# A decoder step's last down projection and final scaling in three token passes of 256, 192 and 128 instead of two of 320 and 256

## The chip, the cores and the metric

One Trainium2 chip, one of its cores. The metric is the device time of one execution in microseconds (us), the median of the runs; an execution also leaves a profile, whose times count from the start of its span. Engines: PE is TensorE (PEld its weight loads), DVE is VectorE, ACT is ScalarE, POOL is GpSimd, SP is SyncE.

## What is computed

One step of a decoder layer for 512 prompt tokens and 8 x 8 sample tokens (576 token columns), model width 1024, feed-forward width 3072, all in float32. The part that the change touches is the end of the layer and the norm behind it:

```
def rmsnorm(x, g):
    xf = x.astype(jnp.float32)
    y = xf * lax.rsqrt(jnp.mean(xf * xf, axis=-1, keepdims=True) + EPS)
    return (y * g.astype(jnp.float32)).astype(x.dtype)
...
    g_conv, new_ffn = causal_dwconv(g_pre, ffn_buf, lw['ffn_conv_w'], lw['ffn_conv_b'])
    h = h + (jax.nn.gelu(g_conv) * val) @ lw['w_down']
...
    y_prompt = rmsnorm(hp, g_final)
    y_sample = rmsnorm(hs, g_final)
```

Ahead of it stand the mixer branches (pooling, a recurrence with gates, cross-attention), their gated merge, and the up projection.

## The kernel before

Activations lie transposed, features on the 128 partitions and tokens along a row, so the model width is 8 tiles of 128 x 576 (`h[0]` to `h[7]`, slices of the one tile `S["h"]`). A float32 product is made of three matmuls of rounded operands (dtype float32r): high by high, high by low, low by high, where `split_to` (L111, L112) makes the high part on ACT and the low part on DVE. In such a matmul the weights are a 128x128 block and the tokens the columns that stream past it; each matmul has its own weight load (PEld).

The feed-forward part (`op_ffn`) runs over 24 tiles of the hidden width. The products of the up projection go into banks of PSUM (`bank()`, four of them, tile `pb`); the down projection is done in six groups of four hidden tiles. For the first five groups `down` (L989) does all 576 tokens in two halves of 288. The last group, `NGR - 1`, has nothing to hide behind and is done in token passes, which the table `FC` names: now columns 0 to 320 and 320 to 576. `last_mm(c, m)` does output tile m of pass c: 4 hidden tiles x 3 matmuls into one bank (L1138), then on DVE the sum with `h[m]` (L1143), on ACT the square of the sum (L277 in `SqSum.add`; L1150 for m = 7) and the scaling by the final norm's weight in place (L1152), and on POOL the running sum of squares (L279).

When a pass has its squares, `fin_cols` calls `rstd_cols`: matmuls with a column of ones, the squares as weights, make the sums over features as one column for each 128 tokens (L241, float32 operands, two matmul records for each instruction in the trace), and small steps on DVE and ACT make the reciprocal root (L245 to L253). `final(c)` spreads the root over the partitions by matmuls with the identity (L1165, float32 too), multiplies `h` by it on DVE, two output tiles at a time (L1172), and stores each result (L1173), in turn from the queues of SP and ACT. Sums, spreads and the bank that they go into come from `pq()`, which has two buffers (tile `pd`).

The order is that of the code, moved a little by the scheduler within the engines. The first pass's root is made and spread within the second pass:

```
        for m in range(8):
            last_mm(0, m)
        for m in range(7):
            last_mm(1, m)
            if m == 1:
                fin_cols(0)
            if m == 3:
                final(0)
        last_mm(1, 7)
        fin_cols(1)
        final(1)
```

Of the kernel before, what the change touches and what calls it, by code (L numbers as in the profile page):

```python
# [11 lines left out]
ALU = mybir.AluOpType  # L12
# [3 lines left out]
P = 128  # L16
# [32 lines left out]
def tile_hybrid_decoder_step(ctx: ExitStack, tc: tile.TileContext, A: dict):  # L49
    nc = tc.nc  # L50
# [16 lines left out]
    def nm(p):  # L67
        uid[0] += 1
        return f"{p}{uid[0]}{cur[0]}"
# [12 lines left out]
    def te(w=UW, dt=F32):  # L82
        if FF:
            return FF["v"].tile([P, T], dt, tag="v", name=nm("v"))[:, :w]
        return ue.tile([P, UW], dt, tag="e", name=nm("e"))[:, :w]
# [7 lines left out]
    def pq():  # L93
        if FF:
            return FF["d"].tile([P, 2, 512], F32, tag="d", name=nm("pd"))[:, 0, :]
        return psp.tile([P, 512], F32, tag="pq", name=nm("pq"), bufs=2)
# [131 lines left out]
    def pc(c):  # L228
        return par[:, c : c + 1]
# [64 lines left out]
    S = {}  # L294
# [428 lines left out]
    h = [None] * 8  # L723
# [23 lines left out]
    def op_ffn():  # L747
# [15 lines left out]
        def bank():  # L763
            return pb.tile([P, 512], F32, tag="b", name=nm("pb"))
# [302 lines left out]
        for j in range(NFF):  # L1067
            pre = j < NPRE
            g, q = j // NFB - 1, j % NFB
            n = j + 1  # L1070
# [53 lines left out]
            WD[last, q] = bt(2 * q, 1024), bt(2 * q + 1, 1024)  # L1124
            split_to(*WD[last, q], r)

        FC = (slice(0, 320), slice(320, 576))

        def last_mm(c, m):
            cs = FC[c]  # L1130
            n = cs.stop - cs.start
            wh, wl = WD[last, m // 2]
            p_ = bank()
            for k in range(NFB):
                xh, xl = prods[last * NFB + k]
                ks = slice((m % 2) * 512 + k * P, (m % 2) * 512 + (k + 1) * P)
                for i, (a, b) in enumerate(((wh, xh), (wh, xl), (wl, xh))):
                    nc.tensor.matmul(  # L1138
                        p_[:, :n], a[:, ks], b[:, cs],
                        start=(k == 0 and i == 0), stop=(k == NFB - 1 and i == 2),  # L1140
                    )
            hc = h[m][:, cs]
            nc.vector.tensor_tensor(hc, p_[:, :n], hc, ALU.add)  # L1143
            if m == 0:
                S["sqf", c] = SqSum(n)
            if m < 7:
                S["sqf", c].add(hc)
            else:
                s7 = te(n)
                nc.scalar.activation(s7, hc, AF.Square)  # L1150
                S["sq7", c] = s7
            nc.scalar.activation(hc, hc, AF.Identity, scale=pc(C_GFIN + m))  # L1152

        def fin_cols(c):
            cs = FC[c]
            S["fr", c] = rstd_cols((S["sqf", c].acc, S["sq7", c]), cs.stop - cs.start)

        def final(c):
            cs = FC[c]
            n = cs.stop - cs.start  # L1160
            r = S["fr", c]
            rl = pq()
            for t in range((n + P - 1) // P):
                w = min(P, n - t * P)
                nc.tensor.matmul(  # L1165
                    rl[:, t * P : t * P + w], r[:w, t : t + 1].to_broadcast([w, P]), ident[:w, :w],
                    start=True, stop=True,
                )
            for q_ in range(4):
                ms = slice(2 * q_, 2 * q_ + 2)  # L1170
                hc = S["h"][:, ms, cs]
                nc.vector.tensor_tensor(hc, hc, rl[:, :n].unsqueeze(1).to_broadcast([P, 2, n]), ALU.mult)  # L1172
                (nc.sync, nc.scalar)[q_ % 2].dma_start(A["yT"][:, ms, cs], hc)  # L1173

        for m in range(8):
            last_mm(0, m)
        for m in range(7):
            last_mm(1, m)
            if m == 1:
                fin_cols(0)  # L1180
            if m == 3:
                final(0)
        last_mm(1, 7)
        fin_cols(1)
        final(1)
        ff.close()


# [146 lines left out]
```

## Time and profile before

| | us |
|---|---|
| median of 3 runs (lowest to highest) | 944.61 (943.54 to 945.12) |
| the profiled execution | 942.23 |
| its span | 940.4 |
| PE busy in the span | 917.6 (98%) |
| DVE, ACT, POOL busy | 621.6, 471.4, 198.7 |
| first matmul of the last group (L1138) to the span's end | 902.2 to 940.4 |

The span is what the trace covers; what lies around it in the profiled execution is 942.23 - 940.4 = 1.8 us. A busy PE is not PE at its peak, since matmuls overlap and their ends are modelled: how fast a stream of matmuls runs is read from the distance of their starts. In a row of the timeline the numbers are the start in the span and the length in us, then engine, line, operation, tiles, shapes and count; in brackets is the idle time of the engine before it and what ended it.

### The profile page before, as it was taken

The page shows a single profiled execution, that of the slowest core. Times are in us where ns is not written, and L with a number is a line of the kernel's source. Part 1 is how long each engine was busy: PE and PEld are TensorE (multiplying, and loading weights), DVE is VectorE, ACT ScalarE, POOL GpSimd, SP SyncE. Part 2 cuts the span into 40 slices and gives each one's busy share as a digit, 9 for nine tenths or more (in the row PEclk, how much of TensorE's full clock was granted, in tenths as well). Part 3 has the DMA queues.
Part 4 walks back from the last instruction along what each step waited for, and adds up shares of the span by engine and source line. Part 5 has one row for each costly group of instructions (what it writes and reads, how often), then busy time and mean ns, then how long its engine had stood idle before and what let it go on. Part 6 is the DMA issues. An engine that isn't in the chain of part 4 may idle for free.

```text
span 940.4 us, 17089 instructions
## 1 busy us (share of the span) xinstructions
PE 917.6 (98%) x6924; PEld 902.1 (96%) x6924; DVE 621.6 (66%) x975; ACT 471.4 (50%) x745; POOL 198.7 (21%) x301
## 2 busy tenths in 40 slices
PE   6999999999999999999999999999999999999996
PEld 6999999999999979899999999999999999999996
DVE  7979864656434666237467998676676676676644
ACT  6455948496222546325455555444444444444443
POOL 5224221127113110012222232111111111111031
PEclk9999999999999999999999999999999999999998
DMA  6422222353232363433636355454454454453203
GB/s 236 141 79 68 70 77 69 95 166 131 87 113 83 124 227 121 175 114 113 223 80 147 100 160 154 125 145 135 125 145 136 127 143 135 126 144 102 90 33 101
DMA packets 39662, 116.73 MB, mean 124 GB/s; under 512 B 4608, under 2 KB 8704, under 8 KB 39584
## 3 DMA queue, kind: packets, MB, share of 16 engines
q1 hardware_dynamic: 34496, 100.19, 31.7%
q0 software_dynamic: 4000, 14.28, 8.7%
q8 instruction: 54, 0.88, 0.4%
q10 hardware_dynamic: 1088, 1.18, 0.4%
q14 instruction: 24, 0.20, 0.1%
HBM read 111.58 MB, written 4.05 MB: 123 GB/s over the span
## 4 chain that ended last, share of the span: by engine, by line
PE 87%; DVE 6%; issue 2%; DMA 2%; ACT 1%; POOL 1%; SPq 0%; POOLq 0%; DVEq 0%; ACTq 0%
PE pb_ffn L903 25%; PE ps_gate L199 15%; PE pd_ffn L989 13%; PE ps_branch L199 11%; PE pb_ffn L808 5%; PE ps_rnn_mm L199 3%; PE ps_q L199 3%; PE pb_ffn L1138 2%; PE ps_pool_mm L199 2%; PE pq_rnn_gate L199 1%; PE pq_k_mm L199 1%; PE ps_v L559 1%; DMA wr_start<-in_w_gate 1%; DMA cv_spv<-in_cv 1%; PE ps_pv L649 1%
## 5 line engine op out<-in xcount | busy, mean ns | idle before, releaser
L903 PE MATMUL pb_ffn<-b_ffn,wh_ffn 128*128 128x288 f32 x768 | 155.2, 295 | 0.0
L903 PEld LDWEIGHTS pb_ffn<-b_ffn,wh_ffn 128*128 128x128 f32 x768 | 123.3, 188 | 0.1
L903 PE MATMUL pb_ffn<-b_ffn,sh_ffn 128*128 128x288 f32 x576 | 119.3, 299 | 2.4 <-DVE b_ffn L112 1.3
L903 PE MATMUL pb_ffn<-b_ffn,wl_ffn 128*128 128x288 f32 x384 | 112.9, 294 | 0.0
L903 PEld LDWEIGHTS pb_ffn<-b_ffn,sh_ffn 128*128 128x128 f32 x576 | 92.1, 188 | 4.4 <-DVE b_ffn L112 1.7
L903 PE MATMUL pb_ffn<-b_ffn,sl_ffn 128*128 128x288 f32 x288 | 84.7, 295 | 0.2 <-DVE sl_ffn L112 0.2
L903 PEld LDWEIGHTS pb_ffn<-b_ffn,wl_ffn 128*128 128x128 f32 x384 | 72.2, 188 | 0.0
L111 ACT ACTIVATE wh_ffn<-wr_ffn 128x1024 fp32r<-128x1024 f32 x44 | 46.7, 1061 | 39.7 <-PE pb_ffn L903 37.7
L111 ACT ACTIVATE sh_ffn<-R_ffn 128x512 fp32r<-128x512 f32 x72 | 45.0, 626 | 26.3 <-PE pb_ffn L903 19.4
L989 PE MATMUL pd_ffn<-xb_ffn,wh_ffn 128*128 128x288 f32 x320 | 55.7, 295 | 1.0 <-ACT xb_ffn L111 1.0
L989 PE MATMUL pd_ffn<-xa_ffn,wh_ffn 128*128 128x288 f32 x320 | 55.7, 296 | 0.0
L903 PEld LDWEIGHTS pb_ffn<-b_ffn,sl_ffn 128*128 128x128 f32 x288 | 54.1, 188 | 0.4 <-DVE sl_ffn L112 0.4
L112 DVE TENSOR_TENSOR wl_ffn<-wr_ffn,wh_ffn 128x1024 fp32r<-128x1024 f32 x44 | 54.1, 1230 | 0.2
L111 ACT ACTIVATE wh_branch<-wr_branch 128x1024 fp32r<-128x1024 f32 (+1 forms) x24 | 22.0, 917 | 62.7 <-PE ps_gate L199 27.2
L976 POOL TENSOR_TENSOR v_ffn<-v_ffn,ext_ffn 128x576 f32<-128x576 f32 x24 | 35.9, 1498 | 79.8 <-ACT ext_ffn L965 77.2
L112 DVE TENSOR_TENSOR sl_ffn<-R_ffn,sh_ffn 128x512 fp32r<-128x512 f32 x72 | 51.3, 713 | 0.5 <-ACT sh_ffn L111 0.5
L112 DVE TENSOR_TENSOR wl_ffn<-R_ffn,wh_ffn 128x1024 fp32r<-128x1024 f32 x22 | 26.9, 1224 | 36.4 <-ACT wh_ffn L111 36.4
L111 ACT ACTIVATE wh_ffn<-R_ffn 128x1024 fp32r<-128x1024 f32 x22 | 23.3, 1060 | 50.7 <-PE pb_ffn L903 47.0
L858 POOL DMA_DIRECT2D wr_ffn<-in_w_up x21 | 18.7, 889 | 142.0 <-DMA wr_ffn<-in_w_up 117.2
L989 PEld LDWEIGHTS pd_ffn<-xb_ffn,wh_ffn 128*128 128x128 f32 x320 | 46.8, 188 | 1.2 <-ACT xb_ffn L111 1.2
L989 PEld LDWEIGHTS pd_ffn<-xa_ffn,wh_ffn 128*128 128x128 f32 x320 | 47.0, 188 | 0.0
L961 DVE SCALAR_TENSOR_TENSOR gc_ffn<-ext_ffn,par,gc_ffn 128x592 f32<-128x592 f32 x48 | 41.4, 863 | 6.1 <-ACT gc_ffn L959 6.1
(510 smaller groups left out, 2428.1 us busy)
## 6 DMA issues: line engine op xcount, KB each, us to landing
R_ffn<-in_w_up SPq DMA_DIRECT2D x24, 512.0 KB, 3.8
wr_ffn<-in_w_down SPq DMA_DIRECT2D x24, 512.0 KB, 3.8
wr_ffn<-in_w_up SPq DMA_DIRECT2D x23, 512.0 KB, 3.7
wr_ffn<-in_w_up POOLq DMA_DIRECT2D x21, 512.0 KB, 6.2
R_ffn<-in_w_up SPq DMA_DIRECT2D x24, 256.0 KB, 4.0
wr_gate<-in_w_gate SPq DMA_DIRECT2D x10, 512.0 KB, 3.3
ck_sscore<-in_ck SPq DMA_DIRECT2D x8, 512.0 KB, 4.4
cv_spv<-in_cv SPq DMA_DIRECT2D x8, 512.0 KB, 5.0
```

Of the source, the lines that this page charges most:

```text
L111: nc.scalar.activation(hi, src, AF.Copy)
L112: nc.vector.tensor_tensor(lo, src, f(hi), ALU.subtract)
L199: nc.tensor.matmul(out[:, c, : hs.stop - hs.start], a[:, ks], b[:, hs], start=(first and k == 0 and i == 0), stop=(last and k == K - 1 and ...
L559: nc.tensor.matmul(vps[:, mt, :], a[:, ms], b[:, ws], start=(k == 0 and i == 0), stop=(k == 7 and i == 2))
L649: nc.tensor.matmul(op[:, e, :256], a[:, hd], b[:, cs], start=(mt == 0 and j == 0), stop=(mt == 1 and j == 2),)
L808: nc.tensor.matmul(p_[:, :TH], a[:, ks], x[:, b], start=(k == 0 and i == 0), stop=(k == 7 and i == 2))
L858: nc.gpsimd.dma_start(SR[j], w2(wu[j][:, 1:3]), accum_op=ALU.add)
L903: nc.tensor.matmul(p_[:, :TH], a[:, ks], b[:, k, :], start=(first and k == 0 and i == 0), stop=(k == 3 and i == 2), skip_group_check=not f ...
L961: nc.vector.scalar_tensor_tensor(gc[:, :592], ext[:, q_ : q_ + 592], pc(cw + q_), gc[:, :592], ALU.mult, ALU.add)
L976: nc.gpsimd.tensor_tensor(v, v, ext[:, :T], ALU.mult)
L989: nc.tensor.matmul(p_[:, c, :TH], a[:, ks], b[:, hs], start=(k == 0 and i == 0), stop=(k == NFB - 1 and i == 2),)
L1138: nc.tensor.matmul(p_[:, :n], a[:, ks], b[:, cs], start=(k == 0 and i == 0), stop=(k == NFB - 1 and i == 2),)
```

## The change

The last group's down projection and the final scaling are done in three passes, of 256, 192 and 128 tokens. `final` is parted: `fin_bcast(c)` spreads the root, `final(c, q_)` multiplies and stores two output tiles. In the code the multiplies of pass 0 stand between the last four outputs of pass 1, those of pass 1 half behind output 4 of pass 2 and half behind the last output, with a second spread of the same root ahead of that half. The stores of passes 0 and 1 go to SP's queue alone, those of pass 2 in turn to SP's and ACT's.

```
-        FC = (slice(0, 320), slice(320, 576))
+        FC = (slice(0, 256), slice(256, 448), slice(448, 576))
...
-        def final(c):
-            cs = FC[c]
-            n = cs.stop - cs.start
+        def fin_bcast(c):
+            n = FC[c].stop - FC[c].start
             r = S["fr", c]
-            rl = pq()
+            S["rl", c] = rl = pq()
             for t in range((n + P - 1) // P):
                 w = min(P, n - t * P)
                 nc.tensor.matmul(
                     rl[:, t * P : t * P + w], r[:w, t : t + 1].to_broadcast([w, P]), ident[:w, :w],
                     start=True, stop=True,
                 )
-            for q_ in range(4):
-                ms = slice(2 * q_, 2 * q_ + 2)
-                hc = S["h"][:, ms, cs]
-                nc.vector.tensor_tensor(hc, hc, rl[:, :n].unsqueeze(1).to_broadcast([P, 2, n]), ALU.mult)
-                (nc.sync, nc.scalar)[q_ % 2].dma_start(A["yT"][:, ms, cs], hc)
+
+        def final(c, q_):
+            cs = FC[c]
+            n = cs.stop - cs.start
+            rl = S["rl", c]
+            ms = slice(2 * q_, 2 * q_ + 2)
+            hc = S["h"][:, ms, cs]
+            nc.vector.tensor_tensor(hc, hc, rl[:, :n].unsqueeze(1).to_broadcast([P, 2, n]), ALU.mult)
+            (nc.sync, nc.scalar if c == 2 else nc.sync)[q_ % 2].dma_start(A["yT"][:, ms, cs], hc)
 
         for m in range(8):
             last_mm(0, m)
-        for m in range(7):
+        for m in range(8):
             last_mm(1, m)
             if m == 1:
                 fin_cols(0)
             if m == 3:
-                final(0)
-        last_mm(1, 7)
-        fin_cols(1)
-        final(1)
+                fin_bcast(0)
+            if 3 < m:
+                final(0, m - 4)
+        for m in range(8):
+            last_mm(2, m)
+            if m == 1:
+                fin_cols(1)
+            if m == 4:
+                fin_bcast(1)
+                final(1, 0)
+                final(1, 1)
+        fin_bcast(1)
+        final(1, 2)
+        final(1, 3)
+        fin_cols(2)
+        fin_bcast(2)
+        for q_ in range(4):
+            final(2, q_)
```

Where the instructions come to stand on an engine is the scheduler's doing. TensorE at the program's end, before: behind the last output's matmuls (`pb`) stand the column sums (L241) and the spread of the root (L1165).

```order
L1138 MATMUL pb_ffn<-xb_ffn,b_1402_ffn 128x256 x2
L1138 MATMUL pb_ffn<-xb_ffn,b_1403_ffn 128x256
L241 MATMUL pd_ffn<-ones,v_ffn 128x1 x4
L1165 MATMUL pd_ffn<-ident,rs_ffn 128x128 x2
L1312 UNCONDITIONAL_BRANCH
```

The same place in the changed program (the spread's line is now L1164):

```order
L1138 MATMUL pb_ffn<-xb_ffn,b_1402_ffn 128x128 x2
L1138 MATMUL pb_ffn<-xb_ffn,b_1403_ffn 128x128
L1164 MATMUL pd_ffn<-ident,rs_ffn 128x128
L1164 MATMUL pd_ffn<-ident,rs_ffn 128x64
L241 MATMUL pd_ffn<-ones,v_ffn 128x1 x2
L1164 MATMUL pd_ffn<-ident,rs_ffn 128x128
L1329 UNCONDITIONAL_BRANCH
```

The second spread of pass 1's root (the first two L1164 rows) stands ahead of the column sums of pass 2, of which there are two instead of four, and one spread instead of two follows. VectorE from the second half of the last pass on, before (L1143 is the sum with `h`, L245 to L253 are the root, L1172 is the final multiply):

```order
L1143 TENSOR_TENSOR h<-pb_ffn,h 128x256
L1172 TENSOR_TENSOR h<-h,pd_ffn 128x2x320 x4
L1143 TENSOR_TENSOR h<-pb_ffn,h 128x256 x4
L245 TENSOR_SCALAR rv_ffn<-pd_ffn 128x2
L250 RECIPROCAL rs_ffn<-rt_ffn 128x8
L251 TENSOR_TENSOR rt_ffn<-rs_ffn 128x8
L252 SCALAR_TENSOR_TENSOR rt_ffn<-rt_ffn,rv_ffn 128x8
L253 SCALAR_TENSOR_TENSOR rs_ffn<-rt_ffn,rs_ffn 128x8
L1172 TENSOR_TENSOR h<-h,pd_ffn 128x2x256 x4
```

And in the changed program (the multiply is L1175):

```order
L1143 TENSOR_TENSOR h<-pb_ffn,h 128x128 x3
L1175 TENSOR_TENSOR h<-h,pd_ffn 128x2x192 x2
L1143 TENSOR_TENSOR h<-pb_ffn,h 128x128 x3
L1175 TENSOR_TENSOR h<-h,pd_ffn 128x2x192 x2
L245 TENSOR_SCALAR rv_ffn<-pd_ffn 128x1
L250 RECIPROCAL rs_ffn<-rt_ffn 128x8
L251 TENSOR_TENSOR rt_ffn<-rs_ffn 128x8
L252 SCALAR_TENSOR_TENSOR rt_ffn<-rt_ffn,rv_ffn 128x8
L253 SCALAR_TENSOR_TENSOR rs_ffn<-rt_ffn,rs_ffn 128x8
L1175 TENSOR_TENSOR h<-h,pd_ffn 128x2x128 x4
```

Two multiplies of pass 1 now stand between the last sum and the root of the last pass. The four multiplies of pass 0 stand in one block, behind the fourth sum of pass 1:

```order
L1143 TENSOR_TENSOR h<-pb_ffn,h 128x192 x2
L1175 TENSOR_TENSOR h<-h,pd_ffn 128x2x256 x4
L1143 TENSOR_TENSOR h<-pb_ffn,h 128x192 x4
L1143 TENSOR_TENSOR h<-pb_ffn,h 128x128 x2
L245 TENSOR_SCALAR rv_ffn<-pd_ffn 128x1
L248 TENSOR_SCALAR rv_ffn<-pd_ffn 64x1
```

The code has them one by one between the outputs; on the engine they are still together, as the block of four of 320 was.

## Rows read from the trace of the kernel before

**Rows 1.** The page: the span, the busy time of PE, and the engines' shares of the chain that ended last.

```profile
span 940.4 us, 17089 instructions
...
PE 917.6 (98%) x6924; PEld 902.1 (96%) x6924; DVE 621.6 (66%) x975; ACT 471.4 (50%) x745; POOL 198.7 (21%) x301
...
PE 87%; DVE 6%; issue 2%; DMA 2%; ACT 1%; POOL 1%; SPq 0%; POOLq 0%; DVEq 0%; ACTq 0%
```

**Rows 2.** The chain that ended last, in order of time, from 902 us on: start us, us, what.

```profile
902.34 16.96 PE pb_ffn L1138 x120
919.30 1.11 PE pd_ffn L241 x12
920.41 3.42 PE pb_ffn L1138 x27
923.83 0.82 PE pd_ffn L1165 x6
...
931.11 1.07 PE pd_ffn L241 x8
...
935.60 1.20 DVE h L1172 x2
```

**Rows 3.** The timeline of PE, 895 to 931 us: the last rows of 288 columns, the first rows of each pass, and the rows around the insertions.

```profile
895.79 0.70 PE L989 MATMUL pd_ffn<-xa_ffn,wh_ffn 128*128 128x288 f32 x4
...
902.18 0.60 PE L1138 MATMUL pb_ffn<-xa_ffn,b_ffn 128*128 128x320 f32 x3
...
916.26 0.52 PE L1138 MATMUL pb_ffn<-xa_ffn,b_ffn 128*128 128x256 f32 x3
...
919.14 1.27 PE L241 MATMUL pd_ffn<-ones,v_ffn 128*128 128x1 f32 x12
920.34 0.62 PE L1138 MATMUL pb_ffn<-xa_ffn,b_ffn 128*128 128x256 f32 x3
...
923.67 0.97 PE L1165 MATMUL pd_ffn<-ident,rs_ffn 128*128 128x128 f32 x6
924.56 0.62 PE L1138 MATMUL pb_ffn<-xb_ffn,b_ffn 128*128 128x256 f32 x3
...
929.70 0.52 PE L1138 MATMUL pb_ffn<-xb_ffn,b_ffn 128*128 128x256 f32 x3
```

**Rows 4.** Busy time by stretch: length, then busy time and instructions of PE, PEld, DVE, ACT and POOL, the granted clock of TensorE, the DMA engines' busy share and GB/s.

```profile
902.18:916.26 14.08, 14.08 (x99) 14.08 (x97) 4.20 (x8) 7.16 (x14) 4.76 (x6) 1.00 0.01 1
...
930.06:940.40 10.34, 1.90 (x14) 1.49 (x12) 3.77 (x10) 1.43 (x4) 0.92 (x2) 0.74 0.32 106
```

**Rows 5.** The timeline of all engines: a sum of 320 columns, the block of multiplies, and the tail from 930 us on.

```profile
904.14 0.49 DVE L1143 TENSOR_TENSOR h<-pb_ffn,h 128x320 f32<-128x320 f32 x1 [1.00 <-PE pb_ffn L1138]
...
924.67 3.02 DVE L1172 TENSOR_TENSOR h<-h,pd_ffn 128x640 f32<-128x640 f32 x4 [0.73 <-PE pd_ffn L1165]
...
930.26 0.42 DVE L1143 TENSOR_TENSOR h<-pb_ffn,h 128x256 f32<-128x256 f32 x1 [1.01 <-PE pb_ffn L1138]
930.78 0.42 ACT L1150 ACTIVATE v_ffn<-h 128x256 f32<-128x256 f32 x1 [0.80 <-DVE h L1143]
...
931.11 0.97 PEld L241 LDWEIGHTS pd_ffn<-ones,v_ffn 128*128 128x128 f32 x8 [1.09 <-POOL v_ffn L279]
...
932.20 0.16 DVE L245 TENSOR_SCALAR rv_ffn<-pd_ffn 128x2 f32<-128x2 f32 x1 [1.52 <-PE pd_ffn L241]
...
933.56 0.52 PEld L1165 LDWEIGHTS pd_ffn<-ident,rs_ffn 128*128 128x128 f32 x4 [1.49 <-issue]
...
934.31 2.48 DVE L1172 TENSOR_TENSOR h<-h,pd_ffn 128x512 f32<-128x512 f32 x4 [0.86 <-PE pd_ffn L1165]
```

**Rows 6.** Weight loads of two lines: count, then shortest, median and longest in ns, first and last start, and the shapes (rows * columns of the array, then the operand).

```profile
L241 PEld LDWEIGHTS pd_ffn<-ones,u_ffn x24: 106/190/192, 472.4 to 499.6; 128*128 128x128 f32 x16, 128*32 128x32 f32 x8
...
L241 PEld LDWEIGHTS pd_ffn<-ones,v_ffn x20: 133/192/192, 919.0 to 931.9; 128*128 128x128 f32 x16, 128*64 128x64 f32 x4
...
L1138 PEld LDWEIGHTS pb_ffn<-xa_ffn,b_ffn x96: 186/188/192, 902.0 to 929.5; 128*128 128x128 f32 x96
```

**Rows 7.** The timeline of PE and PEld behind an idle stretch, at 513.2 us, in the up projection (L903, rounded operands).

```profile
513.26 0.19 PEld L903 LDWEIGHTS pb_ffn<-b_ffn,sh_ffn 128*128 128x128 f32 x1 [1.20 <-DVE b_ffn L112]
513.27 0.40 PE L903 MATMUL pb_ffn<-b_ffn,sh_ffn 128*128 128x288 f32 x1 [0.96 <-DVE b_ffn L112]
513.37 0.19 PEld L903 LDWEIGHTS pb_ffn<-b_ffn,sl_ffn 128*128 128x128 f32 x1
513.50 0.30 PE L903 MATMUL pb_ffn<-b_ffn,sl_ffn 128*128 128x288 f32 x1
513.51 0.19 PEld L903 LDWEIGHTS pb_ffn<-b_ffn,sh_ffn 128*128 128x128 f32 x1
```

**Rows 8.** Groups by line from 902 to 941 us: what each output of a pass costs DVE, ACT and POOL. Busy us, mean ns, then idle time before them.

```profile
L1143 DVE TENSOR_TENSOR h<-pb_ffn,h 128x320 f32<-128x320 f32 (+1 forms) x16 | 7.2, 458 | 15.0 <-PE pb_ffn L1138 15.0
...
L1152 ACT ACTIVATE h<-h,par 128x320 f32<-128x320 f32 (+1 forms) x16 | 8.3, 531 | 0.4
L277 ACT ACTIVATE v_ffn<-h 128x320 f32<-128x320 f32 (+1 forms) x14 | 6.1, 442 | 12.3 <-DVE h L1143 12.3
...
L279 POOL TENSOR_TENSOR v_ffn<-v_ffn 128x320 f32<-128x320 f32 (+1 forms) x12 | 9.7, 807 | 20.7 <-ACT v_ffn L277 20.6
```

**Rows 9.** The DMA engines from 935 to 941 us in 40 slices of 0.15 us (busy tenths, GB/s), and the stores issued there: KB each, median us to landing.

```profile
DMA  0000003999999999999999999991000000000000
GB/s 0 0 0 0 0 0 130 348 307 328 382 348 314 321 362 355 335 301 355 375 348 328 335 362 348 348 307 55 0 0 0 0 0 0 0 0 0 0 0 0
DMA packets 1088, 1.05 MB, mean 175 GB/s; under 512 B 64, under 2 KB 1088, under 8 KB 1088
...
yT<-h ACTq DMA_DIRECT2D x2, 256.0 KB, 2.5
```

**Rows 10.** The timeline of PE in the values' projection (L559), matmuls of 512 columns.

```profile
324.51 0.39 PE L559 MATMUL ps_v<-wl_branch,e_mem 128*128 128x512 f32 x1
324.74 0.39 PE L559 MATMUL ps_v<-wh_branch,e_mem 128*128 128x512 f32 x1
324.97 0.40 PE L559 MATMUL ps_v<-wh_q,e_mem 128*128 128x512 f32 x1
```

## The prediction

> **What bounds the kernel now.** I read the page first. TensorE is busy 98% of the span and holds 87% of the chain that ended last [rows 1], so the kernel is a queue of matmuls, and an edit counts by what it does to that queue and to the stretch after its last matmul. The chain in order of time [rows 2] shows that the edited stretch is of the same kind: from 902 us to the end it is L1138 matmuls with two insertions (L241, the column sums of the squares, and L1165, the spreading of the root), and only behind the last L1138 matmul does it go to VectorE and ScalarE.
>
> The TensorE rows of that stretch [rows 3] give the prices. The pass of 320 tokens starts at 902.18 and the pass of 256 at 916.26: 96 matmuls in 14.08 us, 146.7 ns each. The next 24 matmuls, of 256 columns, take 916.26 to 919.14: 120 ns each. The 48 matmuls of 288 columns from 895.79 to 902.18 take 133 ns each. So a column costs (146.7 - 120) / 64 = 0.417 ns, and 120 - 256 x 0.417 = 13.3 ns is fixed; 288 columns come out at 133.3 by this, as measured. The granted clock is 1.00 there, the 2.4 GHz level, and TensorE has no idle time [rows 4].
>
> The last L1138 rows start at 929.70, three matmuls; the slot of the last ends at 929.70 + 3 x 0.12 = 930.06, which I call E. The span ends at 940.4, E + 10.34, and in that stretch TensorE works 1.90 us [rows 4]: this tail is a chain of short steps [rows 5].
>
> **The change, part by part.**
>
> *Narrower passes.* 8 outputs x 12 matmuls are done for 256, 192 and 128 tokens instead of 320 and 256: 96 matmuls more, the columns the same. The first pass costs what the second costs now, 96 x 0.120 = 11.52 us. No matmul of this kind (both operands rounded, 128x128 weights) under 256 columns is in the trace, so the steps for 192 and 128 columns are to be bounded.
>
> The lower bound is the law above: 93.3 and 66.7 ns. The rows on the weights speak against it. Each matmul has a weight load of its own, and all have 188 ns in the rows, as the f32 loads of 128 columns have (192), while those of 64 columns have 133 and those of 32 have 106 [rows 6]: (188 - 106) / 96 = 0.85 ns a column, 109 ns for 128, over a constant part. Better than these lengths, which a profiler may model, are starts. After an idle stretch at 513.26 a load starts, and the load of the next matmul only at 513.37, 0.11 us later; the first matmul's record is 0.40 us long instead of 0.30, so it stood 0.1 us for its weights [rows 7]. These are operands of the kind that the last passes have. The second matmul then starts at 513.50 and the load of the third at 513.51: one load runs ahead, and it starts when the matmul before it starts. At 256 columns the load is just hidden (109 in 120 ns); below it, the load is the step. The one stream here that is bound by loads is that of the column sums, one column a matmul: 8 loads in 0.97 us, (0.97 - 0.19) / 7 = 111 ns [rows 5].
>
> So I bound the step of the 192- and 128-column matmuls by 111 ns (that stream) and 120 ns (the nearest row by width, if the fixed 13.3 ns come on top of a 107 ns load). I take 111.5, since starting after idle costs both kinds the same 0.11 us: two passes of 96 x 111.5 = 10.70 us. The three passes: 11.52 + 10.70 + 10.70 = 32.93 against 14.08 + 11.52 = 25.60, **+7.3 us** (+9.0 at 120).
>
> *Insertions between the passes.* Now L241 x12 delays the next L1138 matmul from 919.14 to 920.34, 1.20 us, and L1165 x6 from 923.67 to 924.56, 0.89 us [rows 3]. Afterwards there are two of each: column sums of 8 wide loads (8 x 0.111 = 0.9) and of 8 with half of them 64 columns wide (0.8 by 1.20 x 8 / 12), and spreads of 4 records each (0.89 x 4 / 6 = 0.6). 2.9 against 2.09: **+0.8 us**. The insertions wait for nothing as far as I see: ScalarE needs 0.44 + 0.53 us per output, VectorE 0.46, GpSimd 0.81 [rows 8], and the narrow passes give them 12 x 0.1115 = 1.34 us. VectorE's block of four final multiplies in the second pass takes 4 x 0.62 = 2.5 us [rows 5]; TensorE has four banks, of which the block holds up the second pass's last four outputs, and it comes back to the first of these banks four outputs (5.4 us) later. Without that cover the block's rest would stand in TensorE's queue, 2.5 us at most. The first pass's stores move to SP's queue, whose last load is long done; nothing is queued behind them but the stores of the last pass.
>
> *The tail.* Today: the last sum at E + 0.20 for 0.42, the square until E + 1.14, the root's first step on VectorE at E + 2.14 (932.20), the first final multiply at E + 4.25 (934.31), four of them 2.48 [rows 5]. The stores' packets run for 1.05 MB at about 345 GB/s until some 939.3, and the span ends 1.1 later [rows 9]. Afterwards: the sum of 128 columns takes 0.28 (0.49 at 320, 0.42 at 256). The second spread for pass two, 4 records, goes in front of the column sums in TensorE's idle time; VectorE gets it at about E + 0.78 and does two multiplies of 384 elements there (0.755 at 640, 0.62 at 512, so 0.485 each) until E + 1.75. The column sums are 4 records instead of 8 and ready at E + 1.4, so these multiplies are what the root then waits for: its first step is at E + 1.77, 0.37 earlier. From there to the first multiply there are two spread records fewer (0.22): E + 3.66. Then four multiplies of 256 elements (0.35 each) and 0.52 MB of stores, whose rows are 512 bytes where they now have 1 KB. At the present rate they take 1.5 us; if the packets rather than the bytes set it, the present 3.05. I take 2.3. End: 3.66 + 0.41 (first multiply, issue) + 1.0 (issue to first packet, as now) + 2.3 + 1.1 = E + 8.47, **-1.9 us** (-2.7 to -1.1).
>
> Sum: 7.3 + 0.8 - 1.9 = **+6.2 us**. The profiled execution took 942.23 us with a span of 940.4; the median of the runs is 944.61, and I put the change on that: 950.8 us. Bounds: 111.5 ns with the best tail gives +5.4, 120 ns with the worst +8.7.
>
> **The rivals.**
>
> *The loads hide after all* (ends on the other side: not slower). Loads could run further ahead in a stream than after idle, and the 13.3 ns law would hold down to 128 columns: 96 x (93.3 + 66.7) = 15.36 for the two passes, +1.28 + 0.8 - 1.9 = +0.2, 944.8 us. It decides at one number: the mean step of the narrow matmuls must be under (14.08 + 1.1) / 192 = 79 ns. For it: the fixed part is the same from 256 to 320 columns. Against it: the 0.11 us at 513.26 and the 111 ns stream. If the fixed part vanished too (80 and 53 ns), it would be -2.3, 942.3 us; no row shows a rounded matmul without it.
>
> *Between the two.* A stream could hide part of a load: a step of 81 ns at 128 columns and 93.3 at 192 gives 96 x 174.3 = 16.73, +2.65 + 0.8 - 1.9 = +1.6, 946.2 us. For it speaks that what I measured is a start after idle and a stream of f32 operands. Against it speaks the start of each load, which stands at the start of the matmul before it, not earlier. The Trainium skill, "TensorE: Matmul & The Clock Gate", section "Back-to-back issue gap", has such a figure: about 81 ns a matmul for pairs of load and matmul at N=128. By that rule it is this case. The same sentence says about 131 ns for N=512, and this trace has 0.23 us there [rows 10], so I don't let it decide.
>
> *Narrow rounded matmuls run like f32 ones.* The f32 matmuls of the spread take two records of some 0.11 us for 128 columns [rows 5], and the step would be 0.22 us at 128 and 0.33 at 192: 96 x 0.55 = 52.8, +38.7 + 0.8 - 1.9, 982 us. Nothing in the profile shows such a switch, and nothing narrow excludes it.
>
> **How the numbers follow.** Forecast (the load is the step) 0.77; loads hide 0.08; between 0.06; hidden and without the fixed part 0.04; like f32 0.05. A measurement of this kernel can tell about 0.2%, 1.9 us, from no change. So slower is 0.77 + 0.05 = 0.82, same 0.08 + 0.06 = 0.14, faster 0.04. The forecast's own range is 949.5 to 953.5 (the bounds +5.4 and +8.7, and some noise of the median). For 8 in 10 it reaches down through the case between to 945.0; the other three are left out, but for the upper half of the first.
>
> **What the changed profile would show.** Right: the starts of L1138 matmuls 111 to 120 ns apart in both narrow passes, the same for 192 and 128 columns; 10.7 us for each pass without its insertions; the last L1138 slot ending 8 us later than now, and 8 to 9 us from there to the span's end. Wrong: steps that still fall with the width (93, then 67), steps of 200 ns and more, idle time of TensorE among the L1138 matmuls (a bank that is not free), or a tail that stays at 10 us.

## The result: 13 us slower, and the profile after

The changed kernel takes 957.80 us (median of 4 runs, 956.97 to 958.02) against 944.66 beside it, +13.1 us where +6.2 was forecast. The ratio on record is 1.0135 (95% interval 1.0122 to 1.0148); here and below it is not quite the quotient of the two medians. The profiled execution took 956.97 us, 14.7 more than that of before, whose 942.23 was low for its kernel.

The page of the changed kernel, against [rows 1]: the span, PE's busy time, the granted clock in 40 slices (tenths), the shares of the chain.

```profile
span 955.2 us, 17355 instructions
...
PE 934.2 (98%) x7024; PEld 918.2 (96%) x7024; DVE 624.3 (65%) x992; ACT 476.0 (50%) x762; POOL 200.0 (21%) x308
...
PEclk9999999999999999999999999999999999999995
...
PE 88%; DVE 5%; issue 2%; DMA 2%; ACT 1%; POOL 1%; SPq 0%; DVEq 0%; POOLq 0%; ACTq 0%
```

TensorE is as full as before and the chain still runs through it. The one odd sign is the last slice of PEclk. It covers the last 24 us, and a 5 there means that nearly all of it ran at half clock, some 12 us of matmuls included; half clock in the tail's 9.4 us alone would leave an 8.

The timeline of PE, against [rows 3]: the first row of each pass, two steps within the narrow ones, and the insertions (L241, L1164) each with the L1138 row behind it.

```profile
904.36 0.52 PE L1138 MATMUL pb_ffn<-xa_ffn,b_ffn 128*128 128x256 f32 x3
...
915.87 0.48 PE L1138 MATMUL pb_ffn<-xa_ffn,b_ffn 128*128 128x192 f32 x3
...
916.52 0.50 PE L1138 MATMUL pb_ffn<-xa_ffn,b_ffn 128*128 128x192 f32 x3
916.86 0.50 PE L1138 MATMUL pb_ffn<-xb_ffn,b_ffn 128*128 128x192 f32 x3
...
918.53 0.97 PE L241 MATMUL pd_ffn<-ones,v_ffn 128*128 128x1 f32 x8
919.36 0.56 PE L1138 MATMUL pb_ffn<-xa_ffn,b_ffn 128*128 128x192 f32 x3
...
922.11 0.63 PE L1164 MATMUL pd_ffn<-ident,rs_ffn 128*128 128x128 f32 x4
922.49 0.56 PE L1138 MATMUL pb_ffn<-xa_ffn,b_ffn 128*128 128x192 f32 x3
...
927.92 0.47 PE L1138 MATMUL pb_ffn<-xa_ffn,b_ffn 128*128 128x128 f32 x3
...
928.55 0.50 PE L1138 MATMUL pb_ffn<-xa_ffn,b_ffn 128*128 128x128 f32 x3
928.89 0.50 PE L1138 MATMUL pb_ffn<-xb_ffn,b_ffn 128*128 128x128 f32 x3
...
930.56 0.88 PE L241 MATMUL pd_ffn<-ones,v_ffn 128*128 128x1 f32 x8
931.37 0.56 PE L1138 MATMUL pb_ffn<-xa_ffn,b_ffn 128*128 128x128 f32 x3
...
934.83 0.84 PE L1138 MATMUL pb_ffn<-xb_ffn,b_ffn 128*128 128x128 f32 x3
935.47 0.84 PE L1138 MATMUL pb_ffn<-xa_ffn,b_ffn 128*128 128x128 f32 x3
...
936.75 1.35 PE L1164 MATMUL pd_ffn<-ident,rs_ffn 128*128 128x128 f32 x4
938.03 0.90 PE L1138 MATMUL pb_ffn<-xa_ffn,b_ffn 128*128 128x128 f32 x3
...
945.13 0.84 PE L1138 MATMUL pb_ffn<-xb_ffn,b_ffn 128*128 128x128 f32 x3
```

Read the distances, not the lengths. Three matmuls of 192 columns take 916.86 - 916.52 = 0.34 us, three of 128 columns 928.89 - 928.55 = 0.34 as well: over longer stretches 111.7 ns each, the same for both widths. That is the forecast. But at 934.83 the same matmuls take 0.64 us for three, 213 ns each, and stay there to the end. The last slot ends at 945.13 + 0.64 = 945.77.

Windows, against [rows 4]: the 128-token pass up to 933.99, from there to its end, and the tail (length; busy time of PE, PEld, DVE, ACT, POOL; granted clock; DMA share; GB/s).

```profile
927.92:933.99 6.07, 6.07 (x57) 6.04 (x56) 2.15 (x10) 3.12 (x10) 1.05 (x3) 1.00 0.00 0
933.99:945.77 11.78, 11.78 (x55) 11.44 (x55) 2.18 (x6) 2.95 (x9) 2.08 (x5) 0.50 0.12 35
945.77:955.20 9.43, 3.06 (x11) 2.37 (x11) 3.58 (x12) 0.92 (x3) 0.00 (x0) 0.50 0.34 97
```

6.07 us into the pass the granted clock falls from 1.00 to 0.50, from the 2.4 GHz level to the 1.2 GHz level, although TensorE has no idle time before it (6.07 of 6.07). Before the change it fell only at 935.0, in the tail, whose mean in [rows 4] is 0.74. The counts say the same: 57 records in 6.07 us, then 55 in 11.78.

The tail, against [rows 5]: the second spread, the column sums, pass 1's two multiplies, the root's first step, the last spread and the first final multiply.

```profile
945.77 1.35 PE L1164 MATMUL pd_ffn<-ident,rs_ffn 128*128 128x128 f32 x4
...
947.05 1.01 PE L241 MATMUL pd_ffn<-ones,v_ffn 128*128 128x1 f32 x4
...
947.16 1.02 DVE L1175 TENSOR_TENSOR h<-h,pd_ffn 128x384 f32<-128x384 f32 x2 [0.86 <-PE pd_ffn L1164]
...
948.17 0.16 DVE L245 TENSOR_SCALAR rv_ffn<-pd_ffn 128x1 f32<-128x1 f32 x1
...
949.56 0.77 PE L1164 MATMUL pd_ffn<-ident,rs_ffn 128*128 128x128 f32 x2 [1.50 <-DVE rs_ffn L253]
...
950.37 1.41 DVE L1175 TENSOR_TENSOR h<-h,pd_ffn 128x256 f32<-128x256 f32 x4 [0.95 <-PE pd_ffn L1164]
```

The root's first step stands 2.40 us behind the last slot (forecast 1.77), the first final multiply 4.60 (3.66), the end 9.43 (8.47): a gain of 0.9 over the 10.34 of before, not 1.9. The spread in front takes 1.28 us at half clock (945.77 to 947.05).

Of the 14.8 us between the two spans, 13.5 lie in the stretch of L1138 (41.41 against 27.88) and -0.9 in the tail; the other 2.2 us are the later start, 904.36 against 902.18. That part is not the change's, since the code ahead of the last group is the same: this execution had the clock at 0.50 from 26.05 to 29.46 us, and the profiled one of before had not (one window of each):

```profile
27.00:28.00 1.00, 1.00 (x6) 1.00 (x6) 1.00 (x10) 0.10 (x1) 0.02 (x1) 0.50 0.62 238
```

```profile
25.00:30.00 5.00, 5.00 (x40) 4.98 (x39) 4.23 (x24) 2.55 (x4) 0.10 (x1) 1.00 0.73 213
```

3.4 us at half clock cost up to 1.7 us; the rest is of the size by which starts differ without it (902.91 in e6 below, whose clock stayed at 1.00 there). Executions of one kernel seem to differ in this early piece, the likely reason why the medians lie 13.1 apart and these two profiles 14.7.

### The profile page after: what moved, and what is told of

It reads as the page before. It is cut to its first block, busy times and chain, and to the rows that moved or that the text cites. A ratio compares the mean times of both kernels' runs of the same rounds, so it can differ in the third digit from the quotient of the medians.

```text
span 955.2 us, 17355 instructions
## 1 busy us (share of the span) xinstructions
PE 934.2 (98%) x7024; PEld 918.2 (96%) x7024; DVE 624.3 (65%) x992; ACT 476.0 (50%) x762; POOL 200.0 (21%) x308
## 4 chain that ended last, share of the span: by engine, by line
PE 88%; DVE 5%; issue 2%; DMA 2%; ACT 1%; POOL 1%; SPq 0%; DVEq 0%; POOLq 0%; ACTq 0%
PE pb_ffn L903 25%; PE ps_gate L199 15%; PE pd_ffn L989 13%; PE ps_branch L199 11%; PE pb_ffn L808 5%; PE pb_ffn L1138 4%; PE ps_rnn_mm L199 3%; PE ps_q L199 3%; PE ps_pool_mm L199 2%; PE pq_rnn_gate L199 1%; PE pq_k_mm L199 1%; PE ps_v L559 1%; DMA wr_start<-in_w_gate 1%; DMA cv_spv<-in_cv 1%; PE ps_pv L649 1%
## 5 line engine op out<-in xcount | busy, mean ns | idle before, releaser
L903 PE MATMUL pb_ffn<-b_ffn,wh_ffn 128*128 128x288 f32 x768 | 155.3, 296 | 0.0
L903 PEld LDWEIGHTS pb_ffn<-b_ffn,wh_ffn 128*128 128x128 f32 x768 | 123.4, 188 | 0.1
L903 PE MATMUL pb_ffn<-b_ffn,sh_ffn 128*128 128x288 f32 x576 | 119.3, 299 | 2.3 <-DVE b_ffn L112 1.3
L903 PE MATMUL pb_ffn<-b_ffn,wl_ffn 128*128 128x288 f32 x384 | 113.0, 295 | 0.0
L903 PEld LDWEIGHTS pb_ffn<-b_ffn,sh_ffn 128*128 128x128 f32 x576 | 92.1, 188 | 4.4 <-DVE b_ffn L112 1.7
L903 PE MATMUL pb_ffn<-b_ffn,sl_ffn 128*128 128x288 f32 x288 | 84.8, 295 | 0.2 <-DVE sl_ffn L112 0.2
L903 PEld LDWEIGHTS pb_ffn<-b_ffn,wl_ffn 128*128 128x128 f32 x384 | 72.3, 188 | 0.0
L903 PEld LDWEIGHTS pb_ffn<-b_ffn,sl_ffn 128*128 128x128 f32 x288 | 54.1, 188 | 0.4 <-DVE sl_ffn L112 0.4
```

The lines of the kernel that those rows point to most:

```text
L903: nc.tensor.matmul(p_[:, :TH], a[:, ks], b[:, k, :], start=(first and k == 0 and i == 0), stop=(k == 3 and i == 2), skip_group_check=not f ...
```

## The experiments

Beside each group of runs the kernel before took 944.9 to 945.0 us (15 runs each).

**e1_pad256.** The third pass streams 256 columns, of which only the last 128 are used.

```
+ PAD = 128
...
+ lead = PAD if c == 2 else 0
+ ws = slice(cs.start - lead, cs.stop)
...
- p_[:, :n], a[:, ks], b[:, cs],
+ p_[:, : n + lead], a[:, ks], b[:, ws],
...
- nc.vector.tensor_tensor(hc, p_[:, :n], hc, ALU.add)
+ nc.vector.tensor_tensor(hc, p_[:, lead : n + lead], hc, ALU.add)
```

> The third pass streams the columns 320 to 576 past its weights, as the kernel before does, and uses only the last 128 of the 256; everything else is the changed kernel. It does 96 x 128 columns more work. Theory (the clock falls because 128 columns a weight load leave the array idle half of the time): the granted clock stays at 1.00 up to the last sum, the third pass runs at 120 ns a matmul, 11.5 us and its insertions 1.4 instead of the 17.9 us of the changed kernel, the tail gains about 1 us: 952 us, 6 us faster with more work. Rival (the clock falls because of the four insertions, or because narrow matmuls, of whatever width, have run for 18 us): it falls at about 934 us all the same, a step of 213 ns, 958 us.

950.46 us (949.24 to 952.16, 4 runs), 1.0067 times before (1.0052 to 1.0081). Twice the columns in the last pass, and 7 us faster than the changed kernel. Steps of 120 ns, and the clock at 1.00 throughout that pass; then the first final multiply:

```profile
926.14:939.28 13.14, 13.14 (x111) 12.92 (x110) 4.34 (x16) 6.07 (x18) 2.83 (x7) 1.00 0.10 31
...
942.87 1.42 DVE L1179 TENSOR_TENSOR h<-h,pd_ffn 128x256 f32<-128x256 f32 x4 [0.64 <-PE pd_ffn L1168]
```

**e2_192x3.** Three passes of 192.

```
- FC = (slice(0, 256), slice(256, 448), slice(448, 576))
+ FC = (slice(0, 192), slice(192, 384), slice(384, 576))
```

> Three passes of 192, 192 and 192 tokens; code otherwise that of the changed kernel. Theory (the weight load is the step, 111.5 ns at any width under 256, and 192 columns keep the clock): 3 x 10.7 = 32.1 us of matmuls and 2.9 of insertions against 27.9 before, a tail about 1 us shorter than before: 951 us, clock at 1.00 to the last sum. Rival (a stretch that is bound by loads loses the clock whatever its width, later than at 128): it falls some 18 us after the first narrow matmul, half of the stretch runs at 213 ns: about 966 us.

951.0 us (949.27 to 951.82, 4 runs), 1.0069 (1.0055 to 1.0082). The same 288 matmuls, now all 111.7 ns apart but for the insertions, 35 us of them, and the clock held to the last (here the end of the stretch):

```profile
926.00:938.70 12.70, 12.70 (x114) 12.48 (x112) 4.80 (x16) 6.97 (x18) 3.59 (x6) 1.00 0.10 32
```

So a stream whose step is bound as in the forecast does not by itself lose the clock.

**e3_one_spread.** Without the second spread of pass 1's root.

```
-        fin_bcast(1)
         final(1, 2)
```

> The changed kernel without the second spread of pass 1's root; the last two multiplies of pass 1 read the first spread. If the second spread stands in the tail's way (1.28 us of TensorE at the half clock ahead of the column sums, and two multiplies that wait for it), the tail is 0.7 us shorter: 957.1. If it hides in the wait for the last square, no difference: 957.8. The clock falls as in the changed kernel in either case; if it fell earlier, the extra spread would be something that holds it.

956.4 us (955.0 to 957.57, 4 runs), 1.0128 (1.0114 to 1.0142); the changed kernel's interval overlaps it. Two of the four took 955.0 and 955.5 with a mean clock of 0.989, two 957.3 and 957.6 with 0.987 and 0.986, so most of the 1.4 us between the medians seems to be the early piece of half clock, which the profile of e3 (955.0) hasn't. The profile tells more: the last slot ends at 944.49, and

```profile
946.17 0.16 DVE L245 TENSOR_SCALAR rv_ffn<-pd_ffn 128x1 f32<-128x1 f32 x1 [1.15 <-PE pd_ffn L241]
...
948.37 1.42 DVE L1175 TENSOR_TENSOR h<-h,pd_ffn 128x256 f32<-128x256 f32 x4 [0.95 <-PE pd_ffn L1164]
```

the root's first step comes 1.68 us behind it instead of 2.40: the second spread does stand ahead of the last root, for 0.7 us at half clock. The clock fell as in the changed kernel, 5.9 us into the 128-token pass.

**e4_two_pass.** The changed code with the old widths; the third pass and what stands in it go with them.

```
- FC = (slice(0, 256), slice(256, 448), slice(448, 576))
+ FC = (slice(0, 320), slice(320, 576))
...
```

> The changed kernel's code (spread and multiplies parted, the first pass's stores on SP's queue alone) with the two passes of before, 320 and 256. If all of the loss is the widths: TensorE's stretch as before, 27.9 us, and 944.7 within half a us, perhaps 0.3 less where the block of multiplies is broken up and the running sum on GpSimd comes earlier. If the new order or the stores on one queue cost something by themselves, it is slower by what they cost, 1 us or more.

944.86 us (943.15 to 946.91, 11 runs), 1.0000 (0.9989 to 1.0011). Parting the multiplies and moving the first stores to one queue costs and gives nothing; the whole loss belongs to the three passes and what stands in them.

**e5_reverse.** The narrow pass first.

```
+ FC = (slice(0, 128), slice(128, 320), slice(320, 576))
```

> The three passes in the order 128, 192, 256. Theory (a stream of 128-column matmuls, each bound by its weight load, lets the granted clock fall; wider ones give it back): the clock falls about 6 us after the first L1138 matmul, near 908.5 us of the span, and 42 or so matmuls of the first pass then start 213 ns apart instead of 111.7 (+4.3 us). Without any loss of clock this order would be 953: 11.5 + 2 x 10.7 + 2.9 us of stretch against 27.9 and a tail as before. So 957 to 958 us if the clock returns at the start of the pass of 192, 962 if it returns in its middle (48 x 0.1 us), 967 if only with the 256 columns. Rival (not the 128 columns but the length of all narrow streaming, or the place near the program's end, lets it fall: 17.8 us after the first matmul under 256 columns): it falls near 920 us, in the pass of 192 or of 256, and the first pass runs at 111.7 ns throughout.

952.12 us (951.24 to 953.36, 4 runs), 1.0079 (1.0065 to 1.0093): a miss for both theories. There is no fall anywhere in the stretch, and the time is the 953 without any loss of clock. The pass of 128:

```profile
904.66:915.32 10.66, 10.66 (x98) 10.66 (x97) 2.81 (x9) 4.98 (x14) 2.59 (x6) 1.00 0.01 2
```

96 matmuls in 10.66 us, 111 ns each, at full clock. So 128 columns do not lose the clock by themselves either. In this order the pass differs from the changed kernel's in two ways: no narrow pass stands ahead of it, and no insertion stands in it. Three later runs (e8, e9, e10) part these.

**e6_pad192.** As e1, but with 64 columns of padding.

```
- PAD = 128
+ PAD = 64
```

> The third pass streams 192 columns (64 of them of the pass before, their products unused). Theory (128 columns a load let the clock fall, 192 keep it; under 256 the step is the load): L1138 matmuls 111.7 ns apart to the last, granted clock 1.00 until TensorE has nothing more to do, the last slot about 8 us later than before, 949.5 to 951 us, 0.8 us under the padding to 256. Rival (only a stream that hides its loads keeps the clock): the clock falls inside the third pass, and the time is that of the changed kernel, 957 to 958 us.

949.61 us (949.28 to 950.51, 4 runs), 1.0054 (1.0039 to 1.0069); as the theory had it. This run is the changed kernel as it was forecast, since a step costs the same for 128 and 192 columns. The first matmul starts at 902.91, and at the other end:

```profile
938.50 0.50 PE L1142 MATMUL pb_ffn<-xb_ffn,b_ffn 128*128 128x192 f32 x3
...
938.83 0.77 PE L1168 MATMUL pd_ffn<-ident,rs_ffn 128*128 128x128 f32 x4
...
940.57 0.15 DVE L245 TENSOR_SCALAR rv_ffn<-pd_ffn 128x1 f32<-128x1 f32 x1
...
942.75 1.41 DVE L1179 TENSOR_TENSOR h<-h,pd_ffn 128x256 f32<-128x256 f32 x4 [0.95 <-PE pd_ffn L1168]
```

A stretch of 902.91 to 938.83, 35.92 us (forecast 35.8), the root's first step at 1.74 (1.77), the first multiply at 3.92 (3.66), the span's end at 947.6, 8.77 behind the last slot (8.47). Against this span the changed kernel's is 7.6 us longer: 5.5 in the stretch, 0.7 in the tail, both under half clock, and 1.4 of later start.

**e8_mid128.** Passes of 256, 128, 192: insertions in the narrow pass, a wide pass ahead.

```
+ FC = (slice(0, 256), slice(256, 384), slice(384, 576))
```

> Passes of 256, 128, 192: the pass of 128 follows a wide one and holds the insertions (column sums of one column, spread). With the next two runs it tells what, beside 128 columns, the fall of the granted clock needs, since a pass of 128 directly behind 288 columns and without insertions kept 1.00. Theory A (insertions among 128-column matmuls): the clock falls in this pass, some 6 us after its start, and the time is 955 us or more (at least 40 matmuls at 213 instead of 111.7 ns). Theory B (the narrow pass ahead of it, together some 18 us of load-bound matmuls): it stays at 1.00, and the time is that of three passes of 192, 951 us.

The four executions took 951.73, 964.19, 959.34 and 950.94 us, with mean granted clocks of 0.995, 0.981, 0.987 and 0.995. Judged by these, two lost the clock and two did not, so the ratio (1.0145, 1.0093 to 1.0198) is a mixture and no measure. The profile is one of those that kept it, 1.00 from 902 to 942 us, although the column sums stand in it where they stand in the changed kernel, 2.6 us into the pass of 128. Theory B, by which all four should have kept it, falls; theory A holds in two. The slowest lost 13 us against these, more than the pass of 128 can lose behind its column sums (72 matmuls x 0.1 us and a spread, some 8 us): an estimate by which half clock lasted into the pass of 192 behind it, though 192 columns did not let the clock fall in e2 and e6.

**e9_192_128_256.** A narrow pass ahead, insertions inside, a wide pass behind.

```
+ FC = (slice(0, 192), slice(192, 320), slice(320, 576))
```

> Passes of 192, 128, 256: the pass of 128 follows a pass of 192, as in the changed kernel, and holds insertions; 256 columns follow instead of the program's end. Theories A (insertions) and B (a narrow pass ahead) both have the clock fall in the pass of 128, near 6 us after its start, and the time at 956 us or more; if it falls, the matmuls of 256 show whether it comes back. Theory C (it takes the end of the program, whatever it is there): no fall, 952 us as for the order 128, 192, 256.

960.90, 959.57, 953.64 and 959.36 us, mean clocks 0.985, 0.987, 0.994 and 0.987: by these, three of four lost it, so theory C falls. The timeline of PE in one that did; the pass of 128 starts at 915.51:

```profile
918.16 0.88 PE L241 MATMUL pd_ffn<-ones,v_ffn 128*128 128x1 f32 x8
...
920.03 0.50 PE L1138 MATMUL pb_ffn<-xb_ffn,b_ffn 128*128 128x128 f32 x3
920.36 0.74 PE L1138 MATMUL pb_ffn<-xa_ffn,b_ffn 128*128 128x128 f32 x3
920.90 0.84 PE L1138 MATMUL pb_ffn<-xb_ffn,b_ffn 128*128 128x128 f32 x3
...
922.82 1.35 PE L1164 MATMUL pd_ffn<-ident,rs_ffn 128*128 128x128 f32 x4
...
934.40 0.95 PE L1138 MATMUL pb_ffn<-xa_ffn,b_ffn 128*128 128x256 f32 x3
935.15 0.84 PE L1138 MATMUL pb_ffn<-xb_ffn,b_ffn 128*128 128x256 f32 x3
935.79 0.84 PE L1138 MATMUL pb_ffn<-xa_ffn,b_ffn 128*128 128x256 f32 x3
...
937.64 0.52 PE L1138 MATMUL pb_ffn<-xb_ffn,b_ffn 128*128 128x256 f32 x3
937.99 0.52 PE L1138 MATMUL pb_ffn<-xa_ffn,b_ffn 128*128 128x256 f32 x3
```

The clock falls at 920.5, behind the column sums and ahead of the spread (so also in the changed kernel: 930.56, 933.99, 936.75). It lasts through all that is left of the pass of 128 and comes back at 937.5, 3.1 us into the matmuls of 256. At half clock these take 0.64 us for three, as those of 128 do.

**e10_late_insert.** The changed kernel's widths and order of passes, with pass 1's column sums, spread and multiplies behind the last L1138 matmul.

```
             last_mm(2, m)
-            if m == 1:
-                fin_cols(1)
-            if m == 4:
-                fin_bcast(1)
-                ...
+        fin_cols(1)
         fin_bcast(1)
+        final(1, 0)
+        final(1, 1)
         final(1, 2)
```

> The changed kernel's passes (256, 192, 128), but pass 1's column sums, spread and multiplies all stand behind the last L1138 matmul, so that the pass of 128 is matmuls of 128 columns alone. Its time is not compared with the others' (the tail carries some 4 us more); the clock is read. Theory A (insertions): 1.00 until the last L1138 matmul, steps of 111.7 ns throughout, some 953 us. Theory B (a narrow pass ahead): it falls some 6 us into the pass of 128 as in the changed kernel, steps of 213 ns from there, 958 us or more.

951.49 us (951.27 to 953.68, 4 runs), 1.0080 (1.0066 to 1.0094): 6 us faster than the changed kernel although the tail carries a whole root more (12.1 us from the last slot to the end). Mean clocks 0.992 to 0.996. The first two passes, then the pass of 128:

```profile
903.37:926.93 23.56, 23.56 (x207) 23.56 (x205) 9.74 (x25) 14.15 (x32) 7.71 (x13) 1.00 0.14 46
926.93:937.62 10.69, 10.69 (x99) 10.69 (x97) 2.40 (x8) 5.96 (x17) 2.71 (x7) 1.00 0.01 2
```

The pass is 10.69 us long where 10.70 was forecast. It has a pass of 192 directly ahead and no insertion, and it keeps the clock: theory B falls here too, theory A holds. The run moves column sums, small steps, spread and multiplies together, so it doesn't tell which of them matters.

**e7_swap and e11_swap2.** A version that needs no narrow stream. The first 448 tokens go in one pass of 448 columns, and for the last 128 tokens the operands are swapped: the tokens are the 128x128 weights, `w_down` streams 256 columns a matmul. The tokens then stand on partitions, so the squares' sums come from ScalarE's accumulator and the root is a column that needs no spread. (Both runs have the loops and the stores changed to fit, and read the final norm's weight once more, spread over the partitions.)

```
+ FC = (slice(0, 448),)
...
+ nc.tensor.matmul(v2(p_[:, :256]), a, b[:, :, k, :], ...)   # a: tokens 448 to 576, b: w_down
...
+ nc.scalar.activation(tu()[:, :256], p_[:, :256], AF.Square, accum_out=ss[:, q : q + 1])
...
+ nc.vector.scalar_tensor_tensor(o, pB[q][:, :256], r, gb[:, ws], ALU.mult, ALU.mult)
```

> Two passes: 448 tokens as before, then the last 128 tokens with the operands swapped: the tokens are the 128x128 weights, and w_down streams 256 columns a matmul, so that the load is hidden and the stream is wide; tokens then stand on partitions, and the last root is a column of 128 that needs neither column sums nor a spread on TensorE. Worked out: 96 x 200 ns + 48 x 120 ns + 8 f32 matmuls with the identity that add h (1.8 us) + insertions 2.6 = 29.5 us of stretch against 27.9, and a tail of 6.3 us against 10.3 (accumulated squares, 7 small steps of 0.1 to 0.2, a multiply of 256 columns, 0.5 MB of stores): -2.4 us, 942.5 us (941 to 944). The clock stays 1.00 until the last L1138. Rival (the multiplies and stores of the 448 tokens, 1.8 MB, which now come late, end last; or the small steps cost 0.4 us each as in the tail before): 945 to 946.5 us, no gain.

943.57 us (942.07 to 944.76, 11 runs), 0.9986 (0.9978 to 0.9995). In this run `h` was added at the head of each block by two start matmuls into one bank, which by the rule in the last section leaves out the `h` of four of the eight output tiles for these tokens; the matmuls are as many and as wide as if it did not. TensorE also stood for ScalarE once, where two blocks shared a bank:

```profile
933.06 0.71 PE L1139 MATMUL pb_ffn<-ident,h 128*128 128x128 f32 x4 [0.56 <-ACT u_ffn L1151]
```

In e11 each block has its own bank, `h` is added after the first three matmuls, and the column sums stand earlier.

> The swapped last 128 tokens again: h is now added after the first three matmuls of a bank instead of ahead of them, each of the four blocks of 256 outputs has a bank of its own (in the run before, TensorE stood 0.56 us for the square of the block that shared its bank), and the column sums of the 448 tokens stand earlier. Theory: the stretch loses the 0.56 us, the multiplies of the 448 tokens (4 x 1.05 us on VectorE) then end with the last block, 0.2 to 0.5 us less in all: 943.2 us, ratio 0.998. Rival (the multiplies end last and hold the last root): no gain over the run before, 943.6; or 944.9 if the earlier column sums make TensorE wait for ScalarE's square.

942.24 us (941.75 to 943.92, 11 runs) against 945.01: 0.9977 (0.9968 to 0.9986), 2.8 us between the medians, the one version that does the whole work and beats both kernels. Not all of that need be the new version's doing. Eight of its executions have a mean clock of 0.998 or 0.999 and took 941.8 to 942.8 us, three 0.996 or 0.997 and took 943.4 to 943.9; of the kernel before, six had 0.996 or 0.997 and took 943.0 to 944.4, nine 0.995 or less and took 944.8 to 946.6. If the early piece of half clock parts these groups, as the profiles suggest, like against like gives some 1.4 to 1.8 us, and the rest is that the piece came in fewer executions; whether the new version does that is open. Its windows, the pass of 448 and the swapped block:

```profile
903.25:922.71 19.46, 19.46 (x99) 18.04 (x97) 5.13 (x8) 8.74 (x14) 6.56 (x6) 1.00 0.00 1
922.71:933.20 10.49, 10.49 (x89) 10.23 (x87) 4.92 (x11) 4.16 (x10) 0.36 (x1) 1.00 0.13 48
```

The stretch is 29.95 us, 2.1 longer than the 27.88 of before; the tail is 940.2 - 933.20 = 7.0 us, 3.3 shorter than 10.34: 1.3 us to the good. The last multiplies on VectorE follow the small steps directly, with no TensorE between them:

```profile
933.91 0.16 DVE L1156 TENSOR_REDUCE rv_ffn<-sB_ffn 128x1 f32<-128x4 f32 x1
...
935.31 1.66 DVE L1166 SCALAR_TENSOR_TENSOR u_ffn<-pb_ffn,rs_ffn,wr_ffn 128x256 f32<-128x256 f32 x4
```

## Why the prediction was wrong

Its own steps, on the profiles of the two kernels:

| step | forecast | measured |
|---|---|---|
| pass of 256, without insertions | 11.52 | 11.51 |
| pass of 192 | 10.70 | 10.84 |
| **pass of 128** | **10.70** | **15.76** |
| four insertions | 2.9 | 0.83 + 0.38 + 0.81 + 1.28 = 3.30 |
| stretch of L1138 | 35.8 | 41.41 |
| last slot to the span's end | 8.47 | 9.43 |

**The step that failed** is "two passes of 96 x 111.5 = 10.70 us" for the second of these passes. The text read a granted clock of 1.00 off the passes of 320 and 256 columns ([rows 4] shows the first) and, without saying so, kept it for a pass of 128 with column sums in it. No row of before showed a narrow rounded matmul at all, so the clock of such a stream was one of the unknown things to be bounded from both sides, and it stood in neither bound. 120 ns was put down as the worst step; it was 213, past the 200 ns that the text itself named as a sign of being wrong.

The rest of that step held. At full clock the step is the same for both widths: 111.7 ns for 192 and for 128 columns, in the changed kernel until 933.99, in e2 for 35 us, in e10 for the whole pass (10.69 us). That this floor is the weight load fits all of it, but no run varies the load, so the cause of the floor stays argued. The *loads hide* rival needed under 79 ns and is out, with its variant without the fixed part. *Between the two* is out as well: the Trainium skill, "TensorE: Matmul & The Clock Gate", section "Back-to-back issue gap", gives about 81 ns at N=128, and these operands show 111.7; the measurement decides. *Like f32* is out: its 0.22 us are near the 213 ns, but these come and go with the clock, not with the width (e5, e10), and 192 columns took 111.7.

**What lets the clock fall.** The runs exclude the stream at that floor as such (e2, e6), the 128 columns as such (e5, e10), the narrow pass ahead as a needed condition (e8, two of four) and the program's end (e9). What all falling kernels share is one-column matmuls (L241) inside a stream of 128-column ones: four executions of four in the changed kernel (mean clock 0.986 to 0.987) and in e3 (0.986 to 0.989), three of four in e9, two of four in e8. Without them in that pass it fell in none of e5's and e10's eight (0.992 to 0.996), and with 192 or 256 columns around them in none of e1's, e2's and e6's twelve (0.995 to 0.999). Only one execution of each kernel has a trace; the others are counted by time and mean clock, and the lowest of the eight, 0.992, was also seen in the kernel before. The column sums are thus what goes with the fall, not shown to be what makes it: no run moves them alone, and in the kept execution of e8 they stand at the same place. The spread is not needed: it comes after the fall. The Trainium skill, on the same page, section "What's actually happening", has the gate fall to half rate after idling. Here TensorE shows 6.07 us of work in 6.07 us ahead of the fall, so a full PE row is no sign that the clock will stay. The same section of the Trainium skill says of a kernel's start that the gate's stretches of time run freely, so that the number of slow matmuls there differs from run to run. The two of four and three of four are of that kind, but no run here shows it to be the reason; why e8 and e9 sometimes keep the clock stays open.

**The size.** By e6, whose clock stayed, the fall costs 5.5 us of the stretch and 0.7 of the tail, near the whole distance from 950.8 forecast to 957.8. The small miss that is left in the tail lies ahead of the first multiply, 0.26 us later in e6 than forecast. That is the clock again: e6's last spread runs at half clock and takes 0.77 us, while e1's takes 0.46 at 1.00, and its first multiply stands at 942.87 - 939.28 = 3.59 where 3.66 was forecast. From there to the end it is 4.85 us in e6 where 4.8 was put down. That sum was partly luck: the packets ran for 1.9 us, not 2.3, and the end came 1.5 us behind the last of them, not 1.1.

**Where insertions and tail were right.** Insertions at full clock took 0.83, 0.38 and 0.81 us, 2.0 together against 2.3. TensorE had no idle time among the changed kernel's L1138 matmuls, so the four banks covered the multiplies as forecast. The second spread does not only fill idle time: in e6 it holds TensorE from 938.83 to 939.52, and the column sums start right behind it; at half clock the root came 0.7 us earlier without it (e3). What it costs at full clock no run shows.

## What to carry to other kernels

Do not cut a stream of matmuls below the width at which its step stops falling (here between 192 and 256 columns): a narrower matmul costs nearly what one of 256 does (111.7 against 120 ns) and gives less. Where a narrow pass can't be avoided, keep one-column matmuls out of it or pad it: here 64 useless columns bought back 8 us between the medians, 6.2 of it in the stretch and the tail. A step time read at one clock level holds for another stream only if that stream keeps the level, so a forecast of a narrower stream needs a case at half clock; and here a short tail was better bought by swapping operands, so that the narrow dimension became the weights, than by streaming less.

## What the runs showed of the hardware that was not expected

- The clock fell with TensorE busy without a gap: after 6.07 us of a pass of 128 columns in the changed kernel, 5.9 in e3, 5.0 in e9.
- At half clock a matmul of 128 columns takes 213 ns, and one of 256 takes 213 too (0.64 us for three of either in e9); at full clock they take 111.7 and 120.
- It came back by itself 3.1 us into the matmuls of 256 (e9), though not within 14 us of the 128-column stream ahead of them.
- Executions differ by a piece of half clock near 26 us, in code that all these kernels share (26.05 to 29.46 in the changed kernel's profile, none in that of before), worth up to 1.7 us.
- In e7 two start matmuls into one bank stand ahead of each sum. The Trainium skill, "PSUM — Partial Sum Buffer", section "The four PSUM rules", says that a start matmul clears the written marks of the whole bank, so that the next sum there overwrites: by this the first of the two is lost. The run agrees with it, and no run here isolates it; e11 has one start matmul for each bank and does the whole work.
